# One accumulation for the attention and HGRN output products, both GLA heads of a pair together, value products in batches of two, and stores issued with a margin

## The chip, the cores and the metric

The kernel runs on one core of one Trainium2 chip. The metric is the device time of the program in microseconds (us), the median of several runs. PE is the matrix engine, DVE the vector engine, ACT the scalar engine, POOL the GpSimd engine; SP issues the DMAs.

## The reference

A two-layer encoder over 1024 tokens of width 1024. In each layer one input projection feeds four branches (attention with rotary positions, HGRN2, Mamba-2 SSD, GLA), each 512 wide and multiplied by a SiLU gate. One output projection and a layer norm close the layer.

```python
for i in range(DEPTH):
    h = jnp.einsum('bsd,dn->bsn', x, w_in[i])
    (a_q, a_k, a_v, a_z, h_q, h_ff, h_fb, h_i, h_z,
     s_xbc, s_dtf, s_dtb, s_z, g_q, g_k, g_v, g_lf, g_lb, g_z) = split_columns(h, IN_SPLITS)
    y_a = attention_branch(a_q, a_k, a_v, a_z, ...)   # 8 heads of 64, 2 key heads, softmax
    y_h = hgrn2_branch(h_q, h_ff, h_fb, h_i, h_z, ...)   # gated scan, 4 heads, key width 128
    y_s = ssd_branch(s_xbc, s_dtf, s_dtb, s_z, ...)   # conv of 5, chunked scan, 8 heads
    y_g = gla_branch(g_q, g_k, g_v, g_lf, g_lb, g_z, ...)   # gated scan, 4 heads, key width 64
    mixed = jnp.concatenate([y_a, y_h, y_s, y_g], axis=-1)
    out = jnp.einsum('bsn,nd->bsd', mixed, w_out[i])
    x = layer_norm(DEEPNORM_ALPHA * x + out, ln_g[i], ln_b[i])
```

All scans run forward and backward and are summed. GLA's four heads have keys of width 64, so two of them share a tile of 128 partitions: such a pair is what the code calls `p`, and `hh` is the head within it.

## The kernel before

Features lie on the partitions and tokens along the free dimension, in two halves (`hf`) of 512 tokens. A float32 product of the projections is split into a high and a low part (`xh`, `xl`, `whi`, `wlo`; `mxh`, `mxl` for the output projection) and done as three products of 128x512: high with high, high with low, low with high. A weight tile comes by DMA (`wraw`, three buffers), ACT makes `whi` from it and POOL makes `wlo` (`w_conv`, line 458).

Nothing is placed by a scheduler outside the file. `Plan` (line 125) holds a table of costs in ns for each engine, `run` (line 548) goes through the program with it and decides at each step what is emitted next. There are two kinds of items: *fill* items (`F`: input projections and output projections, a queue in order) and *mix* items (`M`, on twelve lanes: attention, scans, norms, loads). An item is a generator; what it yields says what its next step waits for: tiles, free buffers (`"k2:12"` is twelve free buffers of the pool `k2`, 62 of 128x512; `k4`, eight of 128x1024; `"P"` and `"A"` are PSUM banks) or a condition. `run` takes the mix step that is ready first by the plan's clock; where none is ready, or where PE has streamed fewer columns in the present 3413 ns than `share` of 3072 (`behind`, line 143; `share` is the third number of `KNOBS`), it takes a fill step instead. So fill work is what stands between the steps of a chain, and the order is fixed when the program is built: each engine runs its list in order and waits by semaphores.

The stages of a layer, in order: the projections of attention, then attention (`a_qprep`, `a_s`: scores `S` and their maximum `mx` on DVE; `a_e`: scores again as `ST`, exponentials `Pt` on ACT, their running sum `psum` on POOL, line 1621; `a_pv`: products `O` with the values, one key block `st` at a time, line 1651); HGRN's four heads (`h_proj` as fill, `h_mix`); SSD (`spec_proj` and `spec_post` make the decay rates for SSD and GLA, `s_conv`, `s_w`, `s_mix`); GLA's two pairs (`g_load`, `g_mix`); the layer norm. HGRN and GLA share `tree` (line 605: seven levels, each a step on DVE and ACT between products `lv`) and `scan_unit` (line 678), whose `rest` sums three products per chunk `c` of 128 tokens into `ot`: the values with `AT`, and the states `Sb` and `Sf` with `QP`. It does so for one head `hh` after the other (lines 725 to 738); for GLA the second kind of product uses 64 rows of the array.

The output projection is cut by branch `br` (0 attention, 1 HGRN, 2 SSD, 3 GLA) and half. `out_prep` (line 845) loads a branch's result and splits it, at most two of these at a time (`len(mixes) < 2`); `out_proj` (line 868) is fill: four weight tiles `jp`, each for two output tiles `j`, each 12 products of 128x512 (`oproj`). Each branch is added on DVE to the accumulator `acc` in SBUF. Branch 3 takes `A` banks, the others (`OBIG`) a `P` bank.

SP issues all DMAs in order. A result is not stored at once: `store` puts it in a list, and `flush` (line 423) issues those whose source is ready by the plan's clock, ahead of the next step; a load of stored data flushes what it needs.

Of the kernel before, what the change touches and what calls it, by code (L numbers as in the profile page):

```python
# [15 lines left out]
ALU = mybir.AluOpType  # L16
# [21 lines left out]
OA = ((0, 0), (1, 0), (0, 1), (1, 1), (2, 0), (2, 1), (3, 0), (3, 1))  # L38
# [75 lines left out]
TICK, TICK_COLS = 3413.3, 3072.0  # L114
LAT = {("dve", "dve"): 127.0, ("act", "dve"): 131.0, ("dve", "act"): 128.0, ("dve", "pool"): 155.0, ("pool", "dve"): 134.0,
# [9 lines left out]
class Plan:  # L125


    def __init__(self):
# [9 lines left out]
        self.port = []  # L138

# [115 lines left out]
class Eng:  # L255
# [3 lines left out]
    def __getattr__(self, fn):  # L259
        real = getattr(self._e, fn)  # L260

        def call(*args, **kw):
# [7 lines left out]
            if fn == "matmul":  # L270
                cost = n / 2.4 + 13.5 if args[1].dtype == F32R else n / 0.6 + 8.0
                cols = n * args[1].ap[0][1] / 128.0 * (1 if args[1].dtype == F32R else 2)
                if n == 32:
                    cost = 34.0
                elif out.ap[0][1] == 64:
                    cost /= 2
# [28 lines left out]
def hybrid_trunk(ctx, tc, xT_d, wt_d, wo_d, pk_d, w2_d, gain_d, masks_d, imask_d, tri_d, ident_d, rope_d, lnr_d, out_d):  # L305
# [372 lines left out]
    def scan_unit(halves, nh, emit_o):  # L678
# [38 lines left out]
        def rest():  # L717
# [4 lines left out]
            for hf in (0, 1):  # L722
                u = un[hf]
                yield from states(hf, 0, Sf[hf * 4], Sf)
                for hh in range(nh):
                    p = slice(hh * kk, (hh + 1) * kk)
                    yield ["A:1"] + u["AT"] + [S[hf * 4 + c] for S in (Sf, Sb) for c in range(4) if S[hf * 4 + c] is not None]
                    ot = tps("ot")
                    for c in range(4):
                        g = hf * 4 + c  # L730
                        parts = [(halves[hf][1][hh][:, ck(c)], u["AT"][hh][:, ck(c)])]
                        if Sb[g] is not None:
                            parts.append((Sb[g][p, :], u["QP"][p, 1, ck(c)]))
                        if Sf[g] is not None:
                            parts.append((Sf[g][p, :], u["QP"][p, 0, ck(c)]))
                        for n, (a, b) in enumerate(parts):
                            mm(ot[:, ck(c)], a, b, n == 0, n == len(parts) - 1)
                    yield from emit_o(hf, hh, ot)
# [44 lines left out]
    def layer(li):  # L783
# [84 lines left out]
        def out_proj(br, hf):  # L868
# [1103 lines left out]
```

## Time and profile before

| | us |
|---|---|
| median of 3 runs (2640.47 to 2652.59) | 2641.02 |
| the profiled execution | 2644.85 |
| its span, from the first to the last instruction | 2643.0 |
| DVE busy | 1588.1 (60%) |
| POOL busy | 1227.7 (46%) |
| ACT busy | 1092.9 (41%) |

Stages of the first layer by the trace, from the span's start: projections for attention to 130 us, attention to 400, HGRN to 726, SSD to 990, GLA to 1190, the rest of the output projection and the norm to 1350. The second layer follows in the same way and ends at 2643. A row of the view by stretches gives, for each stretch, the busy time and the instructions of each engine, the clock granted to PE (1.00 is full, 0.50 half) and the share of the DMA engines. In the view by groups a row reads: line, engine, operation, output<-inputs, form, count, busy time, mean ns of one, idle time of the engine before them and what ended it. A float32 product that isn't split stands as two records. Nearly every instruction has line 299, the helper that records them, so groups are told apart by their tiles.

### The profile page before, as it was taken

The page shows a single profiled execution, that of the slowest core. Times are in us where ns is not written, and L with a number is a line of the kernel's source. Part 1 is how long each engine was busy: PE and PEld are TensorE (multiplying, and loading weights), DVE is VectorE, ACT ScalarE, POOL GpSimd, SP SyncE. Part 2 cuts the span into 40 slices and gives each one's busy share as a digit, 9 for nine tenths or more (in the row PEclk, how much of TensorE's full clock was granted, in tenths as well). Part 3 has the DMA queues.
Part 4 walks back from the last instruction along what each step waited for, and adds up shares of the span by engine and source line. Part 5 has one row for each costly group of instructions (what it writes and reads, how often), then busy time and mean ns, then how long its engine had stood idle before and what let it go on. Part 6 is the DMA issues. An engine that isn't in the chain of part 4 may idle for free. (4 is left out here: it accounts for less than half of the span.)

```text
span 2643.0 us, 46508 instructions
## 1 busy us (share of the span) xinstructions
PE 2481.6 (94%) x18352; PEld 1855.2 (70%) x18352; DVE 1588.1 (60%) x2895; ACT 1092.9 (41%) x2100; POOL 1227.7 (46%) x932
## 2 busy tenths in 40 slices
PE   8999899999989997889989999999999999988996
PEld 6855457777877886667777655577777787866675
DVE  2574520565489778863555745206664898868737
ACT  4445453332464433334344444533334543433342
POOL 3556663223335446423554566642223454564334
PEclk9999999999989998989999999999999899999998
DMA  6311112011137447622343111120111365676232
GB/s 210 100 48 52 36 43 66 33 53 49 46 112 252 148 148 256 218 71 89 100 162 112 64 38 48 51 68 29 57 41 46 131 237 152 189 262 203 79 104 100
DMA packets 170173, 284.38 MB, mean 108 GB/s; under 512 B 17780, under 2 KB 43380, under 8 KB 169956
## 3 DMA queue, kind: packets, MB, share of 16 engines
q1 hardware_dynamic: 169956, 281.41, 32.5%
q8 instruction: 145, 2.38, 0.4%
q14 instruction: 72, 0.59, 0.1%
HBM read 205.39 MB, written 75.96 MB: 106 GB/s over the span
## 5 line engine op out<-in xcount | busy, mean ns | idle before, releaser
L299 POOL TENSOR_TENSOR wlo<-wraw,whi 128x512 fp32r<-128x512 f32 x372 | 509.9, 1391 | 585.3 <-ACT whi L299 528.7
L299 PE MATMUL proj<-xh,whi 128*128 128x512 f32 x1056 | 429.4, 407 | 4.7 <-DVE u L299 4.7
L299 PE MATMUL proj<-xl,whi 128*128 128x512 f32 x1056 | 415.1, 393 | 0.0
L299 PE MATMUL projh<-xh,whi 128*128 128x512 f32 x704 | 287.8, 409 | 10.4 <-ACT whi L299 9.6
L299 POOL TENSOR_TENSOR psum<-psum,Pt 128x1024 f32<-128x1024 f32 x96 | 228.6, 2381 | 128.2 <-ACT Pt L299 123.1
L299 ACT CAST whi<-wraw 128x512 fp32r<-128x512 f32 x372 | 216.6, 623 | 165.0 <-DMA wraw<-in_wt 63.7
L299 PE MATMUL proj<-xh,wlo 128*128 128x512 f32 x1056 | 281.0, 400 | 0.0
L299 PE MATMUL projh<-xl,whi 128*128 128x512 f32 x704 | 280.2, 398 | 0.3 <-DVE xl L299 0.3
L299 PEld LDWEIGHTS proj<-xh,whi 128*128 128x128 f32 x1056 | 199.6, 189 | 49.1 <-ACT ga L299 5.5
L299 PE MATMUL oproj<-mxh,whi 128*128 128x512 f32 x512 | 217.8, 425 | 15.9 <-ACT whi L299 9.2
L299 PEld LDWEIGHTS proj<-xl,whi 128*128 128x128 f32 x1056 | 200.2, 190 | 37.2
L299 PEld LDWEIGHTS proj<-xh,wlo 128*128 128x128 f32 x1056 | 192.6, 188 | 41.3 <-issue 2.1
L299 ACT ACTIVATE Pt<-ST 128x512 f32<-128x512 f32 x256 | 151.1, 597 | 135.6 <-PE ST L299 133.8
L299 PE MATMUL oproj<-mxl,whi 128*128 128x512 f32 x512 | 206.2, 403 | 0.0
L299 PE MATMUL projh<-xh,wlo 128*128 128x512 f32 x704 | 193.9, 398 | 0.0
L299 DVE TENSOR_REDUCE mx<-S 128x1 f32<-128x1024 f32 x128 | 151.9, 1218 | 53.5 <-PE S L299 52.4
L299 DVE TENSOR_TENSOR QP<-QP,T 128x512 f32<-128x512 f32 x168 | 144.7, 861 | 48.4 <-PE lv L299 47.5
L299 PEld LDWEIGHTS projh<-xh,whi 128*128 128x128 f32 x704 | 134.8, 192 | 54.9 <-issue 13.4
L299 ACT COPY M<-C 128x256 f32<-128x256 f32 x168 | 69.4, 415 | 241.2 <-DVE C L299 241.2
L299 PE MATMUL oproj<-mxh,wlo 128*128 128x512 f32 x512 | 152.7, 412 | 4.1 <-POOL wlo L299 4.1
L299 PEld LDWEIGHTS projh<-xl,whi 128*128 128x128 f32 x704 | 134.9, 192 | 27.5 <-DVE xl L299 1.5
L299 PEld LDWEIGHTS projh<-xh,wlo 128*128 128x128 f32 x704 | 129.0, 189 | 35.3 <-issue 9.7
(241 smaller groups left out, 4602.1 us busy)
## 6 DMA issues: line engine op xcount, KB each, us to landing
wraw<-in_wt SPq DMA_DIRECT2D x244, 256.0 KB
wraw<-in_wo SPq DMA_DIRECT2D x128, 256.0 KB
hdr<-zs SPq DMA_DIRECT2D x64, 256.0 KB
zs<-hdr SPq DMA_DIRECT2D x64, 256.0 KB
bc<-dr SPq DMA_DIRECT2D x64, 256.0 KB
yld<-yd SPq DMA_DIRECT2D x56, 256.0 KB
hdr<-sp SPq DMA_DIRECT2D x40, 256.0 KB
yd<-o SPq DMA_DIRECT2D x40, 256.0 KB
```

The source lines that it names most:

```text
L299: return real(*args, **kw)
```

## The change

The parts, by the functions they touch:

- `out_proj` takes a tuple of branches. Branches 0 and 1 of a half go into one accumulation in one `P` bank, with two weight tiles per `jp`, and one addition to `acc` where there were two. Branch 3 takes a `P` bank too, and `acc` is added after both output tiles of a `jp`. `out_prep` lets four branches be prepared (`NMIX`).
- `scan_unit`'s `rest` takes both heads of a pair in each chunk.
- `a_pv` takes two key blocks per step (`PVB`); `a_e` sums the exponentials on DVE; the number of live `Pt` tiles is `NP` for the first four query blocks and `NQ` = 4 after; `a_pv` has a lane of its own.
- HGRN's first projections may start after query block 4 (`H0`) where it was 6, and a head's mix no longer waits for the last `aP`, but for two free `k4` buffers.
- `spec_proj` comes right after the attention projections and `spec_post` then, where both came after HGRN's projections.
- The first GLA pair starts after SSD's third head pair (`sm2`) where it was the fourth, the second after the fourth where it was the first pair's first half.
- `flush` issues a store only once its source has been ready for 2000 ns by the plan's clock (`LATE`).
- The plan: 95 ns on PE for each change of form (`SWITCH`), new costs for POOL and for small products, `share` 1.0 where it was 0.5.

```diff
-KNOBS = ((None, 100, 0.5),)
-OA = ((0, 0), (1, 0), (0, 1), (1, 1), (2, 0), (2, 1), (3, 0), (3, 1))
+KNOBS = ((None, 100, 1.0),)
+OA = (((0, 1), 0), ((0, 1), 1), ((2,), 0), ((2,), 1), ((3,), 0), ((3,), 1))
+PVB = 2
+H0, NQ = 4, 4
+NMIX = 4
+SWITCH = 95.0
+LATE = 2000.0
...
-                cost = 155 + 2.09 * n + (120 if fn == "tensor_copy" else 0)
+                cost = 160 + 2.17 * n + (120 if fn == "tensor_copy" else 0)
+            if name == "pe":
+                form = (args[1].ap[0][1], out.ap[0][1]) if fn == "matmul" else (128, 128)
+                if form != self._p.form:
+                    cost += SWITCH
+                    self._p.form = form
...
-            if every or key in keys or plan.ready.get(src.tensor.name, 0.0) <= now:
+            if every or key in keys or plan.ready.get(src.tensor.name, 0.0) + LATE <= now:
...
+                yield [f"A:{nh}"] + u["AT"] + [S[hf * 4 + c] for S in (Sf, Sb) for c in range(4) if S[hf * 4 + c] is not None]
+                ots = [tps("ot", hold=True) for hh in range(nh)]
+                for c in range(4):
+                    g = hf * 4 + c
+                    Ss = [(S[g], d) for S, d in ((Sb, 1), (Sf, 0)) if S[g] is not None]
+                    for hh in range(nh):
+                        mm(ots[hh][:, ck(c)], halves[hf][1][hh][:, ck(c)], u["AT"][hh][:, ck(c)], True, False)
+                    for S, d in Ss:
+                        for hh in range(nh):
+                            p = slice(hh * kk, (hh + 1) * kk)
+                            mm(ots[hh][:, ck(c)], S[p, :], u["QP"][p, d, ck(c)], False, d == Ss[-1][1])
...
-                yield [lambda: len(mixes) < 2, f"k2:{OP[li]}"]
+                yield [lambda: len(mixes) < NMIX, f"k2:{OP[li]}"]
...
+        def out_proj(brs, hf):
+                mix = [mixes[br, hf] for br in brs]
+                for jp in range(4):
+                    for i in range(len(brs)):
+                        ws.append(w_get())
...
+                        for jj in range(2):
+                            o, s0 = hs(ps, jj), jj * 128
+                            for n in range(4):
+                                w = whi[:, n * 256 + s0:n * 256 + s0 + 128]
+                                mm(o, w, mix[i][n][0], i == 0 and n == 0, False)
+                                mm(o, w, mix[i][n][1], False, False)
...
-                    yield [lambda: live[0] < NP[li], "k4:1"]
+                    yield [lambda: live[0] < (NP[li] if ti < H0 else NQ), "k4:1"]
...
-                        tt(gp, acc_s, acc_s, P, ALU.add)
+                        tt(ve, acc_s, acc_s, P, ALU.add)
...
+                for s0 in range(0, 8, PVB):
+                    sts = range(s0, s0 + PVB)
+                    yield [lambda: all((ti, st) in pts for st in sts)]
...
+        F(f"sp{li}", spec_proj, after=x1 + [f"set{li}"], ws=[wsrc("sp")])
+        M(f"spp{li}", spec_post, needs=[f"sp{li}"], lane=3)
-        F(f"sp{li}", spec_proj, after=[f"hp{li}3"], ws=[wsrc("sp")])
-        M(f"spp{li}", spec_post, needs=[f"sp{li}", f"hm{li}2"], lane=3)
...
-            M(f"gp{li}{p}", g_load(p), needs=names + ([f"sm{li}3"] if p == 0 else [f"gn{li}0"]), lane=8)
+            M(f"gp{li}{p}", g_load(p), needs=names + ([xlast, f"sm{li}2"] if p == 0 else [f"sm{li}3"]), lane=8)
```

How it moves instructions, at three places. The first is PE in the first layer's GLA, at the sums `ot` of the first pair's first half (the number behind a name is the buffer's). Before, in one of the two heads (`V_9402`), each chunk's product with `AT` is followed by that head's two products with the states:

```order
L299 MATMUL ot_10619<-AT_10267,V_9402 128x128
L299 MATMUL ot_10619<-QP_9410,S_10533 128x128
L299 MATMUL ot_10619<-QP_9410,S_10561 128x128
L299 MATMUL ot_10619<-AT_10267,V_9402 128x128
L299 MATMUL ot_10619<-QP_9410,S_10531 128x128
L299 MATMUL ot_10619<-QP_9410,S_10563 128x128
```

In the changed program the same place reads:

```order
L312 MATMUL ot_10605<-AT_10228,V_9271 128x128
L312 MATMUL ot_10606<-AT_10234,V_9273 128x128
L312 MATMUL ot_10605<-QP_9292,S_10419 128x128
L312 MATMUL ot_10606<-QP_9292,S_10419 128x128
L312 MATMUL ot_10605<-QP_9292,S_10520 128x128
L312 MATMUL ot_10606<-QP_9292,S_10520 128x128
```

Two products of full height now stand together, and the 64-row products of the two heads alternate between two `ot` tiles.

The second place is PE between that pair's sums `ot` of the first and of the second half (`gss` is the sum of squares of a finished head, `kst`, `P` the next states, `lv` a level of the other half's tree). Before, from the second head's sum on:

```order
L299 MATMUL lv<-QP,M 32x32 x32
L299 MATMUL gss<-sq,ones 128x512
L299 MATMUL oproj<-mxh,whi 128x512
L299 MATMUL oproj<-mxl,whi 128x512
L299 MATMUL kst<-ident,M 128x128
L299 MATMUL kst<-ident,C 128x128
L299 MATMUL kst<-ident,M 128x128
L299 MATMUL kst<-ident,C 128x128
L299 MATMUL lv<-QP,M 32x32 x32
L299 MATMUL P<-V,KST 64x128 x6
L299 MATMUL oproj<-mxh,whi 128x512
L299 MATMUL oproj<-mxl,whi 128x512
```

In the changed program, from the products `P` of that place on:

```order
L312 MATMUL P<-V,KST 64x128 x6
L312 MATMUL oproj<-mxh,wlo 128x512 x2
L312 MATMUL oproj<-mxh,whi 128x512
L312 MATMUL oproj<-mxl,whi 128x512
L312 MATMUL oproj<-mxh,whi 128x512
L312 MATMUL oproj<-mxl,whi 128x512
L312 MATMUL oproj<-mxh,whi 128x512
L312 MATMUL oproj<-mxl,whi 128x512
L312 MATMUL oproj<-mxh,whi 128x512
L312 MATMUL oproj<-mxl,whi 128x512
L312 MATMUL oproj<-mxh,wlo 128x512 x4
L312 MATMUL lv<-QP,M 32x32 x32
```

Where two products of the output projection stood between two steps of the chain, fourteen stand now.

The third place is DVE in the first layer's attention, around a query block's score maxima `mx`. Before:

```order
L299 TENSOR_REDUCE mx<-S 128x1 x4
L299 TENSOR_SCALAR qhl<-mx 128x4
L299 SCALAR_TENSOR_TENSOR qhl<-mx,qhl 128x4
L299 TENSOR_REDUCE mx<-S 128x1 x3
L299 TENSOR_TENSOR ya<-O,rz 128x512
L299 TENSOR_REDUCE mx<-S 128x1
```

In the changed program:

```order
L312 TENSOR_REDUCE mx<-S 128x1
L312 TENSOR_TENSOR psum<-Pt 128x1024
L312 TENSOR_REDUCE mx<-S 128x1
L312 TENSOR_TENSOR psum<-psum,Pt 128x1024
L312 TENSOR_REDUCE mx<-S 128x1
L312 TENSOR_TENSOR ya<-O,rz 128x512
L312 TENSOR_REDUCE mx<-S 128x1
```

A sum of 128x1024 now stands between two maxima on the same engine.

More of the change, by code (lines that the diff above doesn't have):

```diff
@@ L138, in __init__ @@
         self.port = []
+        self.form = None
     def warm(self, t):
@@ L273, in call @@
                 if n == 32:
-                    cost = 34.0
+                    cost = 28.0
                 elif out.ap[0][1] == 64:
@@ L724, in rest @@
                 yield from states(hf, 0, Sf[hf * 4], Sf)
-                for hh in range(nh):
[L726 to L738, printed above, removed]
+                yield [f"A:{nh}"] + u["AT"] + [S[hf * 4 + c] for S in (Sf, Sb) for c in range(4) if S[hf * 4 + c] is not None]
[9 more added lines that the diff above has]
+                            mm(ots[hh][:, ck(c)], S[p, :], u["QP"][p, d, ck(c)], False, d == Ss[-1][1])
+                del Ss, S
+                for hh in range(nh):
+                    yield from emit_o(hf, hh, ots[hh])
                 u.clear()
@@ L866, in out_prep @@
             return gen
[L868 removed]
+        def out_proj(brs, hf):
             def gen():
[L870 to L871 removed]
+                mix = [mixes[br, hf] for br in brs]
+                first, final = 0 in brs, 3 in brs
                 for jp in range(4):
[L873 to L885 removed]
+                    ws, xr = [], []
+                    for i in range(len(brs)):
+                        ws.append(w_get())
+                        if i == 0:
+                            yield [ws[0][0]] + [m[0] for m in mix[0]] + [m[1] for m in mix[0]]
+                            if first:
+                                flush([("xd", hf)])
+                                for j in (jp * 2, jp * 2 + 1):
+                                    xr.append(k2("xr"))
+                                    sy.dma_start(xr[-1], xsrc[j * 128:(j + 1) * 128, hf * HALF:(hf + 1) * HALF])
@@ new lines, in gen @@
+                    for jj in range(2):
+                        j, o = jp * 2 + jj, hs(ps, jj)
+                        if first:
+                            a = k2("acc")
+                            acc[j, hf] = a
+                            ve.scalar_tensor_tensor(out=a, in0=xr.pop(0), scalar=ALPHA, in1=o, op0=ALU.mult, op1=ALU.add)
+                        else:
+                            a = acc[j, hf]
+                            tt(ve, a, a, o, ALU.add)
+                        if final:
+                            summed.add((j, hf))
@@ L927, in layer, with o_src @@
+                    drop(ps)
+                    del ws, whi, wlo
+                for br in brs:
+                    del mixes[br, hf]
+            return gen
+        def o_src(brs):
+            return [wo_d[li, br, jp] for jp in range(4) for br in brs]
         h_in, o_h, lbs = {}, {}, {}
@@ L1265, in gen @@
                     yield None
-                sd["g", g] = (Cc, CB, Bt)
+                sd["g", g] = (Cc, Bt)
+                sd["cb", g] = CB
             return gen
@@ L1459, in emit_o @@
                 ac.copy(o, ot)
+                drop(ot)
                 res = []
```

112 lines of the change are left out of this document (34 added, 78 removed).

## The prediction

> **What bounds the kernel now.** I read the page's first part, then the stretches, then PE's waits, then single rows. The page's first rows:
>
> ```profile
> span 2643.0 us, 46508 instructions
> PE 2481.6 (94%) x18352; PEld 1855.2 (70%) x18352; DVE 1588.1 (60%) x2895; ACT 1092.9 (41%) x2100; POOL 1227.7 (46%) x932
> ```
>
> PE is busy 94% of the span, and the two programs hold the same products. So the change can act on four things: what a product costs beside its neighbours, PE's idle time (161 us here), the time in which PE's clock is lower, and the program's ends. Where idle time and clock are lost is read from the stretches:
>
> ```profile
> core 0: us, PE busy (x) PEld busy (x) DVE busy (x) ACT busy (x) POOL busy (x), PEclk, DMA share, GB/s
> 130.00:400.00 270.00, 250.36 (x1046) 143.20 (x1045) 137.38 (x155) 130.72 (x218) 164.47 (x84) 0.98 0.15 47
> 462.00:726.00 264.00, 261.39 (x2767) 206.12 (x2766) 144.50 (x312) 93.41 (x192) 80.16 (x76) 1.00 0.14 45
> 726.00:765.00 39.00, 32.34 (x269) 23.16 (x268) 32.22 (x45) 28.53 (x44) 17.78 (x16) 0.82 0.26 95
> 990.00:1190.00 200.00, 167.29 (x2370) 126.24 (x2372) 152.74 (x292) 68.16 (x131) 96.34 (x83) 0.87 0.55 182
> 1450.00:1720.00 270.00, 259.67 (x1125) 158.21 (x1123) 139.23 (x169) 132.96 (x225) 168.97 (x86) 0.98 0.16 50
> ...
> 2046.00:2112.00 66.00, 61.46 (x422) 47.20 (x421) 57.02 (x81) 40.41 (x62) 26.45 (x22) 0.90 0.35 121
> 2310.00:2460.00 150.00, 129.89 (x1738) 98.19 (x1736) 113.23 (x206) 50.92 (x96) 75.84 (x65) 0.92 0.63 208
> ```
>
> A stretch loses its idle time, and its length times what is missing of the clock. By that, attention loses 20 + 5 = 25 us in layer 1 (first row) and 10 + 5 = 15 in layer 2 (fifth); HGRN 2.6 of 264 (second); the stretch with `spec_post` 7 + 7 = 14 (third) and 5 + 7 = 12 (sixth); GLA 33 + 26 = 59 (fourth) and 20 + 12 = 32 (last). HGRN runs the same tree as GLA and loses 1%: what differs is the fill work between the steps. GLA's 91 us are the largest loss of any stage, and no single cause makes them, as PE's longest waits in the first GLA stretch show (total, times, longest):
>
> ```profile
> PE oproj L299 <- ACT whi L299: 9.2, 1, 9.2
> PE lv L299 <- POOL ks L299: 3.7, 1, 3.7
> PE lv L299 <- DVE QP L299: 3.1, 4, 1.1
> PE oproj L299 <- POOL wlo L299: 2.8, 2, 2.3
> ```
>
> **The change part by part.** The sum is made against the profiled execution, 2644.85 us, which stands 3.8 above the median of the runs, 2641.02.
>
> *A, changes of form on PE.* Counted in the two programs' order, 798 neighbours on PE differ in form (rows times columns of the array) before and 668 after: `O` goes in batches of two, `ot` with both heads, and fill lands elsewhere. The price, from three products behind a 64*64 one:
>
> ```profile
> 1109.08 0.50 PE L299 MATMUL oproj<-mxh,whi 128*128 128x512 f32 x1
> 1109.42 0.40 PE L299 MATMUL oproj<-mxl,whi 128*128 128x512 f32 x1
> 1109.65 0.39 PE L299 MATMUL oproj<-mxh,whi 128*128 128x512 f32 x1
> ```
>
> The first, which follows the change, takes 0.34 to the next start, the second 0.23. I take 0.1 for a change (the difference is 0.11 here): 130 x 0.1 = **-13 us**. This is PE's own list, so nothing hides it.
>
> *B, the 64-row products of two heads in turn.*
>
> ```profile
> 1159.05 0.71 PE L299 MATMUL ot<-QP,S 64*128 64x128 f32 x4
> 1159.69 0.49 PE L299 MATMUL ot<-AT,V 128*128 128x128 f32 x2
> ```
>
> ```profile
> L299 PE MATMUL ot<-QP,S 64*128 64x128 f32 x224 | 45.2, 320 | 0.0
> L299 PE MATMUL lv<-QP,M 128*64 128x64 f32 x512 | 21.9, 228 | 0.0
> L299 PE MATMUL lv<-QP,M 64*64 64x64 f32 x512 | 12.2, 230 | 5.2 <-DVE QP L299 3.8 <-ACT M L299 1.1 <-DVE near L299 0.4
> ```
>
> Four records of one head take 0.64 to the next start, 0.54 without the change of form; 224 records are 56 such fours, 30 us. Whether the upper and the lower 64 rows run side by side on 128 columns no row shows. The nearest is `lv`: as many records take 12.2 us where both row halves are used and 21.9 where one is all 128 rows, a ratio of 0.56. I take that: 0.44 x 30 = **-13 us**, from 0 to -15. The page TensorEngine Tiling (Array Packing) of the Trainium skill, section Restrictions and Gotchas, says that different row tiles must not use one PSUM bank at the same time; the two heads write two `ot` tiles, so by that page they may overlap, and a full halving would make the term -15.
>
> *C, GLA with more fill between its steps.* In layer 1 the first pair's steps had 2 to 4 output products between them, and 186 stood in one block behind GLA; after, 4 to 18 stand between them and 134 in the block. One `oproj` is a step of 0.23 us (above), so a gap of 2 covers 0.5 us and one of 14 covers 3.2, which is more than most of the waits above. HGRN, with 4 to 16 between its steps, loses 1%; at that rate GLA's 350 us would lose 4, the best end, -87. The other end is 0, as DVE is busy 153 of 200 and 113 of 150 us there. Layer 2 had 2 to 20 already. I take 59 to 19 in layer 1 and 32 to 20 in layer 2: **-52 us**. The merging of branches 0 and 1 goes in here; the 32 additions to `acc` that it saves (0.68 each) cost PE nothing now, since DVE waits for them:
>
> ```profile
> L299 DVE TENSOR_TENSOR acc<-acc,oproj 128x512 f32<-128x512 f32 x96 | 62.5, 680 | 64.3 <-PE oproj L299 63.7
> ```
>
> *D, `spec_post` moved into attention.* Its old stretches lose 14 + 12 = 26 us. The chain through ACT and DVE is as long in its new place, where projections stand between its steps. I take half: **-12 us**, from -26 to 0.
>
> *E, attention.* 112 sums of 128x1024 leave POOL (2.38 each, 266 us) and go to DVE. The rows, in ns least, median and most: the sum on POOL with those who waited for it, the same form on DVE (the first `QP`), and the score maximum:
>
> ```profile
> L299 POOL TENSOR_TENSOR psum<-psum,Pt x96: 2337/2377/2611, 147.4 to 1734.9; 128x1024 f32<-128x1024 f32 x96
> ...
> who waited for it (us, times):
>   ACT rz L299: 3.4, 3
>   ACT Pt L299: 0.9, 1
> ```
>
> ```profile
> L299 DVE TENSOR_TENSOR QP<-q,T x24: 1216/1222/2292, 472.4 to 2482.0; 128x1024 f32<-128x1024 f32 x24
> ```
>
> ```profile
> L299 DVE TENSOR_REDUCE mx<-S 128x1 f32<-128x1024 f32 x128 | 151.9, 1218 | 53.5 <-PE S L299 52.4
> ```
>
> Nobody waited 5 us for `psum`, so a faster sum gains little. DVE gets 56 x 1.22 = 68 us per layer, on 137 of 270; the stage also gets longer, as the block of bare projections behind it shrinks from 238 to 114 products (28 us) in layer 1. The cover is DVE's idle half, and the fill between two `S`. What is queued behind a sum on DVE is the maximum of a score tile (1.22), for which PE waits before the next-but-one `S`. At best the stage's 25 + 15 us go; for the worse end see the rivals. I take **0**. The lower limit on `Pt`, the earlier start of HGRN, the added waits for free buffers, and the plan's new constants only set this order, and have the same two ends.
>
> *Stores with a margin: 0.* SP waits long for the sources of stores, with weight loads queued behind:
>
> ```profile
> SPq L299 <- POOL wlo L299: 810.3, 181, 17.2
> SPq L299 <- DVE zs L299: 522.7, 45, 30.7
> ```
>
> But of this PE sees only waits for `whi`, whose one large case (9.2 us) is in C. Loads that flush their own store keep doing so. I keep -10 and +10 as ends.
>
> *F, the end: +2 us.* The last four transposes of 128x128 no longer stand among products: 12 follow the last `oproj`, where 8 did. With the copies (0.28 each, partly side by side) that is about 2 us:
>
> ```profile
> L299 ACT COPY xt<-outT 128x128 f32<-128x128 f32 x64 | 12.4, 280 | 26.0 <-PE outT L299 25.8
> ```
>
> The sum: -13 - 13 - 52 - 12 + 0 + 0 + 2 = -88; 2644.85 - 88 = 2557, and 3.8 lower against the median: **2553 us**.
>
> **The rivals.**
>
> *GLA's chain is bound by DVE, not by missing fill.* For it: DVE is busy about 76% there, and two pairs side by side load it more. Against: HGRN's tree is covered with 4 to 16 products. C would be -15: **2590**.
>
> *The sums on DVE hold up the score maxima (slower).* One queue, one place: each of the 128 `S` tiles finds a sum of 1.22 us ahead of its maximum, PE has two such tiles, and the fill isn't enough. If all are exposed that is 156 us on 2553: **2709**; from 83 tiles on the change is slower by over 0.5%. POOL can make it worse, as single rows of `QP` with the same two inputs reach 2.29, 1.07 above the median. Against it: DVE waits 52 us for `S` now, and the median of that row stands at its least. The page SBUF — State Buffer of the Trainium skill, section Who interferes with whom, says that a DVE instruction with two SBUF inputs and a GpSimd one that reads SBUF exclude each other for the whole instruction; the tail of `QP` agrees.
>
> *The change doesn't do what it says.* Its order is better by the plan's clock, and on the chip the waits reappear elsewhere, attention losing 15 us more: A, B and F stay, 2553 + 52 + 12 + 15 = **2632**, within 0.5%.
>
> *Everything is covered.* C at -87 and 20 of attention's 40 us: **2498**.
>
> **How the numbers follow.** My forecast has 0.55 (its own range is 2525 to 2590), the DVE-bound GLA 0.22, everything covered 0.06, no effect 0.09, slower 0.08. The range of 2510 to 2628 takes in the first two with the bounds of A, B, D and the stores; it leaves out the last two and half of the third, 2 in 10. About 0.5% (13 us) is what a measurement of this kernel can tell from no change. Faster: 0.55 + 0.22 + 0.06 = 0.83; within 0.5%: 0.09; slower: 0.08.
>
> **What would show it.** A: steps behind `O` and `ot` fewer, PE's busy sum lower at a full clock. B: the 64-row `ot` records at about half of their 45 us of busy time. C: in GLA's stretches a clock above 0.95 and idle time under 10%. D: no stretch behind HGRN at 0.82 or 0.90. E: PE's waits for DVE `mx`; if they pass 40 us in total, the step is wrong. The forecast as a whole falls if attention's stretches lose over 40 us each.

## The result, and the profile after

The changed kernel takes **2578.73 us** (median of 4 runs, 2576.8 to 2583.47), the kernel before beside it 2642.85 (2640.47 to 2652.59). The ratio is 0.9753, with a 95% interval of 0.9725 to 0.9782: 64 us faster. Predicted were 2553 us, in a range of 2510 to 2628. The profiled execution took 2583.47 us, 61.4 less than that of before (2644.85).

The first rows of the page of the changed kernel:

```profile
span 2581.4 us, 46457 instructions
PE 2439.2 (94%) x18352; PEld 1843.5 (71%) x18352; DVE 1637.3 (63%) x2975; ACT 1075.9 (42%) x2090; POOL 963.8 (37%) x820
```

PE does the same number of products in 42 us less of busy time, and its idle time fell from 161 to 142 us. POOL lost the 264 us of the sums, DVE got them at half the price. Where the time went is read by stages; the view by stretches of the kernel before, over attention (two rows) and over SSD and GLA together (two rows), which is now cut at the stages' own ends:

```profile
113.00:412.00 299.00, 279.36 (x1179) 162.70 (x1177) 151.88 (x175) 142.07 (x239) 181.39 (x93) 0.98 0.15 46
1444.00:1734.00 290.00, 279.67 (x1212) 170.61 (x1210) 144.76 (x176) 143.30 (x242) 183.21 (x94) 0.98 0.16 51
...
785.00:1231.00 446.00, 406.47 (x3720) 321.64 (x3718) 337.21 (x639) 170.71 (x325) 212.23 (x178) 0.94 0.53 174
2102.00:2554.00 452.00, 422.68 (x3838) 334.20 (x3837) 350.98 (x652) 177.47 (x340) 221.87 (x188) 0.97 0.55 181
```

The same of the changed kernel, with the last stretch of HGRN, where `spec_post` was (740 and 2003), and GLA alone (988 and 2279) among them:

```profile
137.00:457.00 320.00, 312.75 (x1384) 201.85 (x1386) 214.43 (x259) 164.62 (x284) 75.41 (x52) 0.99 0.20 63
1411.00:1724.00 313.00, 308.40 (x1367) 198.22 (x1367) 214.94 (x259) 166.78 (x283) 77.45 (x52) 0.99 0.20 65
...
740.00:779.00 39.00, 36.25 (x258) 29.10 (x257) 28.74 (x53) 14.93 (x27) 8.75 (x10) 0.91 0.42 140
2003.00:2069.00 66.00, 62.70 (x503) 51.57 (x503) 54.18 (x101) 28.37 (x50) 15.36 (x15) 1.00 0.36 126
...
797.00:1188.00 391.00, 362.43 (x3594) 287.87 (x3594) 285.01 (x578) 150.71 (x291) 201.78 (x173) 0.96 0.55 183
2069.00:2489.00 420.00, 383.68 (x3655) 304.42 (x3653) 305.47 (x587) 153.65 (x297) 211.45 (x179) 0.94 0.56 178
...
988.00:1188.00 200.00, 179.38 (x2582) 135.48 (x2582) 141.15 (x251) 75.71 (x141) 101.70 (x92) 0.94 0.50 167
2279.00:2489.00 210.00, 187.05 (x2586) 141.10 (x2584) 135.14 (x249) 68.47 (x128) 93.16 (x87) 0.91 0.43 142
```

A stretch loses its idle time and its length times what is missing of the clock, as in the prediction. Attention lost 26 and 16 us and now loses 10 and 8. SSD and GLA together lost 66 + 43 = 109 us and now lose 44 + 62 = 106: layer 1 won 22, and layer 2 lost 19 again. So the stage that the prediction counted on most gave next to nothing, and attention, counted at nothing, gave 24 us.

The rest of the gain is in what products cost. In the view by groups, of the changed kernel:

```profile
L312 PE MATMUL O<-Pt,Vt 128*64 128x512 f32 x512 | 125.7, 612 | 0.0
L312 PE MATMUL ot<-AT,V 128*128 128x128 f32 x256 | 48.3, 290 | 2.1 <-DVE S L312 2.0
L312 PE MATMUL ot<-QP,S 64*128 64x128 f32 x224 | 22.4, 315 | 0.0
```

The 64-row records of `ot` are busy 22.4 us, where they were 45.2, though one of them lasts as long as before (315 ns, where it was 320): they run two at a time. By the page TensorEngine Tiling (Array Packing) of the Trainium skill, section Restrictions and Gotchas, different row tiles must not use one bank at the same time; the two heads write two tiles, and the trace agrees that these overlap. Those of `O` take 125.7, where they took 137.8:

```profile
L299 PE MATMUL O<-Pt,Vt 128*64 128x512 f32 x512 | 137.8, 624 | 7.0 <-ACT Pt L299 5.1 <-DVE zs L299 1.9
```

The sums on DVE, and the maxima beside them (ns least, median and most):

```profile
L312 DVE TENSOR_TENSOR psum<-psum,Pt x96: 1207/1225/2303, 167.0 to 1722.2; 128x1024 f32<-128x1024 f32 x96
...
L312 DVE TENSOR_REDUCE mx<-S x128: 1205/1216/1226, 139.3 to 1669.7; 128x1 f32<-128x1024 f32 x128
```

The median is what was predicted, and of the tail of 2303 little comes into the mean (1279). PE's longest waits for its chains, and that for `mx` (total, times, longest):

```profile
PE yd L312 <- POOL Wm L312: 12.3, 2, 7.5
...
PE P L312 <- ACT KST L312: 9.8, 3, 4.9
...
PE lv L312 <- DVE near L312: 9.5, 4, 4.4
...
PE S L312 <- DVE mx L312: 0.9, 3, 0.4
```

The sums stand between the maxima, and PE waits 0.9 us for these in the whole program. What waits there are belong to SSD (`yd`) and GLA (`P`, `lv`).

**A second measure.** The experiments were judged by PE's time split in two. Products are sorted by their tiles, their form, and whether the next one has the same form. The price of a sort is the mean distance from one start to the next, over the lower nine tenths of those without a gap and at a full clock. The sum of all prices is PE's *list*; what PE takes beyond it is its *loss* (idle time and slow clock together). By this, the list fell from 2309 to 2267 us, and the loss from 306 to 283: in attention from 70 to 50 (43 to 26 in layer 1, 28 to 24 in layer 2), in SSD and GLA from 143 to 142 (84 to 64, 60 to 78), elsewhere from 92 to 91. One execution is uncertain here: the profiled one of the changed kernel is the slowest of its four (2583.47 us), and the three kernels below that keep its order and GLA's work lose 130 to 135 us in SSD and GLA. So some 10 of the 142 us belong to that execution.

### The profile page after: what moved, and what is told of

The parts are those of the page before. It is cut to its first block, busy times and chain, and to the rows that moved or that the text cites. A ratio compares the mean times of both kernels' runs of the same rounds, so it can differ in the third digit from the quotient of the medians.

```text
span 2581.4 us, 46457 instructions
## 1 busy us (share of the span) xinstructions
PE 2439.2 (94%) x18352; PEld 1843.5 (71%) x18352; DVE 1637.3 (63%) x2975; ACT 1075.9 (42%) x2090; POOL 963.8 (37%) x820
## 5 line engine op out<-in xcount | busy, mean ns | idle before, releaser
L312 POOL TENSOR_TENSOR wlo<-wraw,whi 128x512 fp32r<-128x512 f32 x372 | 518.9, 1416 | 672.3 <-ACT whi L312 609.4
L312 DVE TENSOR_TENSOR QP<-QP,T 128x512 f32<-128x512 f32 x168 | 150.1, 894 | 46.3 <-PE lv L312 44.6
L312 DVE TENSOR_TENSOR psum<-psum,Pt 128x1024 f32<-128x1024 f32 x96 | 122.8, 1279 | 63.7 <-ACT Pt L312 62.9
```

What stands on the lines that cost most here:

```text
L312: return real(*args, **kw)
```

## The experiments

All kernels, with the ratio to the kernel before on the same chip, and, from the trace of one execution each, list and loss. "Against" is the difference of ratios times 2641 us: against the changed kernel (0.9753) in the upper rows, against the kernel before in the last two. A difference to the changed kernel is uncertain by some 10 us, since both ratios have intervals of about 0.003 to each side.

| kernel | median, us | ratio (95%) | against | list | loss | of it attention | SSD + GLA |
|---|---|---|---|---|---|---|---|
| before | 2642.85 | 1 | | 2309 | 306 | 70 | 143 |
| changed | 2578.73 | 0.9753 (0.9725 to 0.9782) | | 2267 | 283 | 50 | 142 |
| heads_apart | 2630.29 | 0.9974 (0.9951 to 0.9997) | +58 | 2295 | 297 | 54 | 151 |
| heads_fixed | 2598.72 | 0.9856 (0.9830 to 0.9883) | +27 | 2294 | 266 | 49 | 130 |
| sums_pool | 2585.90 | 0.9812 (0.9786 to 0.9839) | +16 | 2273 | 287 | 62 | 134 |
| sums_fixed | 2608.19 | 0.9882 (0.9855 to 0.9909) | +34 | 2267 | 308 | 81 | 133 |
| gla_old | 2594.77 | 0.9846 (0.9818 to 0.9873) | +25 | 2271 | 290 | 57 | 142 |
| unmerged | 2592.88 | 0.9817 (0.9800 to 0.9833) | +17 | 2272 | 286 | 62 | 135 |
| late0 | 2575.48 | 0.9750 (0.9733 to 0.9766) | -1 | 2266 | 279 | 48 | 136 |
| yld_margin | 2588.24 | 0.9799 (0.9783 to 0.9815) | +12 | 2274 | 276 | 59 | 122 |
| yld_act | 2573.23 | 0.9747 (0.9724 to 0.9770) | -2 | 2268 | 275 | 50 | 135 |
| gla_short_qp | 2568.60 | 0.9733 (0.9707 to 0.9759) | -5 | 2267 | 264 | 50 | 123 |
| before_heads | 2648.56 | 1.0031 (1.0020 to 1.0043) | +8 | 2280 | 332 | 83 | 154 |
| before_sums | 2642.46 | 1.0025 (1.0009 to 1.0040) | +7 | 2312 | 296 | 50 | 155 |

Most of these edits make the plan choose another order from the edit on, for every engine. Four kernels, `heads_fixed`, `sums_fixed`, `yld_act` and `gla_short_qp`, keep the changed kernel's order: the plan reckons as in the changed kernel, and only what is issued differs.

### The two heads

`heads_apart`:

```diff
-                for c in range(4):
...
-                    for S, d in Ss:
-                        for hh in range(nh):
...
+                for hh in range(nh):
+                    p = slice(hh * kk, (hh + 1) * kk)
+                    for c in range(4):
...
+                        for S, d in Ss:
                             mm(ots[hh][:, ck(c)], S[p, :], u["QP"][p, d, ck(c)], False, d == Ss[-1][1])
```

> The changed kernel, with the products of `ot` given one head after the other again (all of the first head's chunks, then all of the second's), two `ot` tiles still held at once. Up to the first layer's GLA the order is that of the changed kernel. Theory (the gain lies in what products cost on PE beside their neighbours: by the mean distances of starts, the 64-row products with the states went from 36 to 16 us, those with `AT` from 37 to 32): 20 to 28 us are lost again, 2599 to 2607 us, and the 64-row `ot` rows are busy 45 us again, from 22. Rival (the gain comes from the new order of fill and chains, and the heads' order is hidden behind GLA's waits): within 8 us of 2579, whatever those rows show.

The list grew by 28 us as the theory has it, but the time by 52 to 58, far above both expectations. Of the rest, 14 us show in the trace as loss of the new order (10 more in the first layer's GLA and 11 in the second's SSD, with some won elsewhere); the two profiled executions are only 42 us apart. Two causes in one number; so the next kernel keeps the order. `heads_fixed` lets the plan reckon with the heads together, holds the products back, and issues them head by head:

```diff
+                pe._held, heads = [], []
...
-                del Ss, S
+                held, pe._held = pe._held, None
+                for hh in range(nh):
+                    for b, (real, args, kw) in zip(heads, held):
+                        if b == hh:
+                            real(*args, **kw)
```

> The changed kernel with its whole order as it is (every other instruction of every engine in its place); only inside each sum `ot` of GLA are the products given one head after the other. It tells the direct cost of the heads' order from what a new plan brings. Theory (the products are on PE's own list, and what they save is saved in the end): 22 to 30 us lost, 2601 to 2609, the 64-row rows busy 45 us. First rival (GLA's waits take it, as in the kernel before with the heads together, where 28 us less of products gave no time): under 10 us lost, below 2589. Second rival (the 51 us that the heads' order cost with a new plan are its own): over 40 us lost, above 2619.

Its group of 64-row products:

```profile
L760 PE MATMUL ot<-QP,S 64*128 64x128 f32 x224 | 41.8, 301 | 0.0
```

They are back at 41.8 us, the list is 27 us longer, and the time 20 (by medians, a little under the expected range) to 27 us (by ratios). What the order of the heads takes off PE's list is saved in the end; the theory holds, and the excess of `heads_apart` was the order. (Its loss of 266 is that of one execution, 5 us below the median.)

`before_heads` does the same part alone, in the kernel before:

```diff
+                ots = [tps("ot", hold=True) for hh in range(nh)]
+                for c in range(4):
...
+                    for S, d in Ss:
+                        for hh in range(nh):
+                            p = slice(hh * kk, (hh + 1) * kk)
+                            mm(ots[hh][:, ck(c)], S[p, :], u["QP"][p, d, ck(c)], False, d == Ss[-1][1])
...
                 for hh in range(nh):
-                    p = slice(hh * kk, (hh + 1) * kk)
...
-                    ot = tps("ot")
...
-                        for n, (a, b) in enumerate(parts):
-                            mm(ot[:, ck(c)], a, b, n == 0, n == len(parts) - 1)
```

> The kernel before, with nothing changed but both heads of a GLA pair in each chunk of `ot`. Theory (this shortens PE's own list by 20 us at the 64-row products and by 7 at those with `AT`): 20 to 30 us faster than the kernel before, 2613 to 2623, the 64-row rows busy 22 us. Rival (in the old order this time lies beside GLA's waits, which take it back): within 10 us of 2643, with the same rows at 22 us.

The rival holds, and more than it said: PE's list is 29 us shorter, and the kernel is 8 us slower (5 to 11). The loss grew by 26 us, half of it not in GLA but in the second layer's attention, where nothing was edited. Its row, beside which the kernel before has 10 us of idle time:

```profile
1419.00:1722.00 303.00, 281.08 (x1197) 165.89 (x1197) 148.75 (x176) 142.39 (x242) 181.15 (x93) 0.98 0.15 47
```

PE is idle for 22 us there; its longest waits are 7.5 us in all for `Pt` and 6.2 for `qhl`, of the kind that the next part follows back. So the same edit is worth 27 us in one order and nothing in another. Which step of the plan loses the time in the old order wasn't followed up.

### The sums

`sums_pool` (the plan knows of it) and `sums_fixed` (it does not):

```diff
-                        tt(ve, acc_s, acc_s, P, ALU.add)
+                        tt(gp, acc_s, acc_s, P, ALU.add)
```

```diff
+    vg = Eng(plan, "dve", nc.gpsimd)
...
-                        tt(ve, acc_s, acc_s, P, ALU.add)
+                        tt(vg, acc_s, acc_s, P, ALU.add)
```

> The changed kernel, with the sums of the exponentials on POOL again. Theory (attention's loss, which fell from 43 to 26 us in layer 1 and from 28 to 24 in layer 2, fell because a sum of 1.2 us frees `Pt` tiles earlier than one of 2.4): 15 to 25 us are lost again, 2594 to 2604 us, and PE waits more in attention. Rival (the batches of two value products and the lower limit on `Pt` did it, and the engine of the sum is free): within 8 us of 2579, attention losing 25 in each layer.

> The changed kernel with its whole order as it is; only the engine of the sums of the exponentials is POOL, at the same places of the program. Theory (a sum of 2.4 us behind others on POOL frees `Pt` later, and PE waits in attention): 10 to 25 us lost, 2589 to 2604, attention's loss up from 26 and 24 us by as much. Rival (the 7 us that the sums on POOL cost with a new plan came from the plan): within 6 us of 2579.

With a new plan 7 (medians) to 16 us (ratios) are lost, between the two expectations, and attention's loss is 62. In the same order 29 to 34 us are lost, more than the theory asked for, and all of it in attention (loss 50 to 81). The two attention stretches of `sums_fixed`:

```profile
137.00:477.00 340.00, 319.68 (x1385) 205.49 (x1386) 182.95 (x203) 165.09 (x285) 201.60 (x108) 0.97 0.18 59
1430.00:1754.00 324.00, 309.93 (x1362) 198.85 (x1364) 175.05 (x203) 166.81 (x285) 202.25 (x108) 0.99 0.19 63
```

Idle time is 20 and 14 us, where it was 7 and 5, and both stages are longer, by 20 and 11 us. PE's longest waits in the first of them (total, times, longest):

```profile
PE ST L312 <- ACT Pt L312: 7.0, 4, 4.5
PE qmT L312 <- DVE qhl L312: 7.0, 7, 2.0
...
PE Z L312 <- POOL psum L312: 0.6, 1, 0.6
```

The waits for `psum` itself are 0.6 us. What costs more are waits for others, and they lead back to DVE. `qhl` is made by two instructions of DVE on four columns; their durations (ns least, median and most), in the changed kernel and then in `sums_fixed`:

```profile
L312 DVE TENSOR_SCALAR qhl<-mx x32: 170/171/1198, 144.8 to 1671.0; 128x4 fp32r<-128x4 f32 x32
```

```profile
L312 DVE TENSOR_SCALAR qhl<-mx x32: 170/530/2349, 145.2 to 1697.8; 128x4 fp32r<-128x4 f32 x32
```

One of them, of the second kind, in `sums_fixed`:

```profile
359.89 2.35 POOL L312 TENSOR_TENSOR psum<-psum,Pt 128x1024 f32<-128x1024 f32 x1
359.99 2.27 DVE L312 SCALAR_TENSOR_TENSOR qhl<-mx,qhl 128x4 fp32r<-128x4 f32 x1
...
362.41 0.50 PE L312 MATMUL qmT<-ident,qhl 128*128 128x128 f32 x4 [1.99 <-DVE qhl L312]
```

An instruction of 0.17 us starts 0.1 us after a sum on POOL, lasts 2.27 us, and ends with it. Of the 64 of both kinds, 22 take over 0.3 us in `sums_fixed` and 5 in the changed kernel, and each of these ends 22 to 32 ns after an instruction of POOL (in `sums_fixed` a sum for 13 of the 22). The longest wait, 4.5 us for `Pt`, has the same source: ACT, which makes `Pt`, stands 6.9 us for `tot`, the end of `spec_post`'s chain on DVE, and from `RA` to `tot` this chain takes 17.9 us in `sums_fixed`, where it took 9.0. PE's waits of `qmT` for `qhl`, 11.3 us in the whole program where they were 1.0, and this one make up 15 of the 22 us by which PE's idle time in attention grew; the rest was not taken apart. In the whole program no `Pt` on ACT is seen to wait for a sum, so what the expectations named, `Pt` tiles that a slower sum frees later, is not what the trace shows. The page SBUF — State Buffer of the Trainium skill states, in the section Who interferes with whom, that DVE and GpSimd (POOL) share a pair of ports, and that of two instructions that both need it the later one is blocked until the first is done. The trace agrees with it in the instructions named here.

`before_sums` is the same edit in the kernel before, to DVE:

```diff
-                        tt(gp, acc_s, acc_s, P, ALU.add)
+                        tt(ve, acc_s, acc_s, P, ALU.add)
```

> The kernel before, with nothing changed but the sums of the exponentials, which go to DVE. Theory (a faster sum frees `Pt` earlier): 10 to 20 us faster than the kernel before, 2623 to 2633 us, its attention losing less than 43 and 28 us. Rival (without the batches and the lower limit the sums stand in front of the score maxima): equal or slower, 2643 to 2665 us, with PE waiting over 10 us for `mx`.

Attention's loss fell from 70 to 50, just as in the changed kernel, without batches and without the lower limit on `Pt`; PE's waits of `qmT` for `qhl` fell from 7.1 us in the kernel before to 0.3. So the engine of the sums is what shortens attention, and it needs no other part. But the kernel is 7 us slower (2 to 11): the loss of SSD and GLA in the new order is 155, where it was 143.

### SSD and GLA: the loss that stays

`gla_old`:

```diff
-            M(f"gp{li}{p}", g_load(p), needs=names + ([xlast, f"sm{li}2"] if p == 0 else [f"sm{li}3"]), lane=8)
+            M(f"gp{li}{p}", g_load(p), needs=names + ([f"sm{li}3"] if p == 0 else [f"gn{li}0"]), lane=8)
```

> The changed kernel, with GLA's first pair starting after SSD's fourth head pair and its second after the first pair's first half, as in the kernel before. Theory (the earlier start brought nothing: SSD and GLA together lost 84 us before and 64 after in layer 1, 60 before and 78 after in layer 2): within 10 us of 2579, layer 1 losing more and layer 2 less. Rival (what was predicted, that the earlier start and the fill around it save GLA's idle time, and something else in layer 2 took it): 25 to 50 us are lost, 2604 to 2629.

25 us were lost (16 by medians), between the two expectations. By the trace SSD and GLA lose 142 us (73 and 68), as much as in the changed kernel's profiled execution and some 10 more than in other executions of its order, so the start decides little of this loss; 4 us more are in the list and 7 in attention.

The changed kernel's longest wait of PE in these stages is 7.5 us for POOL's `Wm`. The timeline around it (start, length, instruction, and in brackets the idle time before it and its releaser), shown for the engines of that chain:

```profile
2261.66 1.85 SPq L312 DMA_DIRECT2D yld<-yd  x4
...
2265.91 0.62 ACT L312 CAST mxh<-yld 128x512 fp32r<-128x512 f32 x1 [4.89 <-DMA yld<-yd]
...
2268.09 0.62 ACT L312 CAST mxh<-yld 128x512 fp32r<-128x512 f32 x1 [1.56 <-DMA yld<-yd]
...
2268.91 1.33 ACT L312 CAST mxh<-yld 128x512 fp32r<-128x512 f32 x2 [0.20 <-DMA yld<-yd]
...
2270.15 0.62 ACT L312 ACTIVATE sq<-u 128x512 f32<-128x512 f32 x1
2270.68 0.61 ACT L312 ACTIVATE bc<-bc 128x512 f32<-128x512 f32 x1
2270.86 1.27 POOL L312 TENSOR_TENSOR ssq<-ssq,sq 128x512 f32<-128x512 f32 x1 [8.32 <-ACT sq L312]
...
2272.09 1.26 POOL L312 TENSOR_TENSOR u<-u,zs 128x512 f32<-128x512 f32 x1
...
2273.32 1.26 POOL L312 TENSOR_TENSOR Wm<-Wm,bc 128x512 f32<-128x512 f32 x1
...
2274.62 1.75 PE L312 MATMUL yd<-Wm,xt 128*64 128x128 f32 x13 [7.50 <-POOL Wm L312]
```

PE is said to wait for POOL. POOL has stood 8.32 us for ACT's `sq`, does two instructions of its list first, and then `Wm`, for which it also needs ACT's `bc`. ACT could have made both earlier, had not four casts `mxh` for the output projection stood ahead of them, waiting for loads that SP issued at 2261.66. The wait belongs to a load of another stage, at the head of ACT's list. Two kernels test that. `yld_margin` moves the casts back:

```diff
                     sy.dma_start(y, ydr[r0:r0 + 128, hf * HALF:(hf + 1) * HALF])
+                    plan.ready[y.tensor.name] += 6000.0
```

> The changed kernel, in which the plan takes a loaded branch result (`yld`) as ready 6 us later, so that its casts `mxh` on ACT come later in ACT's list. Theory (SSD and GLA lose about 142 us whatever their start, because a cast stands first in ACT's list for a load that is late, 7.5, 4.5 and 4.4 us of PE's waits in layer 2 of the changed kernel): the loss of SSD and GLA falls below 125 us, ACT waits under 10 us for `yld` there, and the time is 2555 to 2570 us. Rival (DVE, busy 72 to 91% in these stages, bounds them): the loss stays at 142 within 10 and the time within 8 us of 2579, with the waits at other places.

The step is nearly as expected, the time not. ACT's waits for `yld` in SSD and GLA are down from 17.0 and 30.7 us to 8.0 and 12.3, where under 10 was expected; PE's wait of 7.5 us for `Wm` in layer 2 is gone, and the loss of SSD and GLA is 122. But attention loses 9 us more, the list is 7 longer, and the kernel is 12 us slower. `yld_act` has ACT issue the same loads, in the same order:

```diff
+    sy, sw = Eng(plan, "dma", nc.sync), Eng(plan, "dma", nc.scalar)
...
-                    sy.dma_start(y, ydr[r0:r0 + 128, hf * HALF:(hf + 1) * HALF])
+                    sw.dma_start(y, ydr[r0:r0 + 128, hf * HALF:(hf + 1) * HALF])
```

> The changed kernel with its whole order on PE, DVE and POOL as it is; only the loads of the branch results (`yld`, 56 of 256 KB) are issued by ACT at the same places of the program, not by SP, which stands up to 18.6 us for the buffers of weight loads. Theory (the casts stand on ACT for loads that SP issued late): ACT's waits for `yld` fall from 51 us to under 25, PE's waits of 7.5, 4.5 and 4.4 us in the second layer's SSD and GLA shrink, and 5 to 15 us are won, 2564 to 2574. Rival (the loads are late because the transfers come in bursts that fill the DMA engines, or DVE bounds these stages): within 6 us of 2579, ACT's waits within a third of 51 us.

The rival holds: the same time (ratio 0.9747). ACT waits 47.8 us for `yld` where it waited 51.5, only in more and shorter pieces:

```profile
ACT mxh L312 <- DMA yld<-yd: 47.8, 33, 4.5
```

At the place shown above ACT stands for a weight tile first, issues the loads at 2266.39, and waits 3.96 us for the first of them. So it is not SP's list alone that makes these loads late.

`gla_short_qp` takes work off DVE in GLA's chain:

```diff
+            ve._held = [] if nh == 2 else None
             tt(ve, qa, qa, AV(T, nblk + 1, [[2, ng2], [-nblk - 1, 2], [0, h]]), ALU.mult)
+            ve._held = None
+            if nh == 2:
+                qs = QP[:, 1, 0:64]
+                nc.vector.tensor_tensor(out=qs, in0=qs, in1=AV(T, 0, [[0, 64]]), op=ALU.mult)
```

> The changed kernel with its whole order as it is; only in GLA's tree is the scaling of `QP` on DVE done on 64 columns in place of 512, so that most of `QP` is left without its decay factors. 56 instructions of DVE, one at each level, are shorter by some 0.55 us at least, 31 us in all, on the chain from one level to the next. Theory (GLA's steps are bound by its chain through DVE, which is busy 72 to 79% there): GLA's loss of 46 and 55 us falls by 15 us or more in total, and 12 to 31 us are won, 2548 to 2567. Rival (fill covers the level-to-level steps, and GLA's loss sits at single waits behind loads and other stages' work, and in the clock that follows them): under 8 us won, above 2571, with PE's waits of 4 us and more where they were.

The rows of that scaling in the changed kernel, and then in this one (HGRN's and GLA's):

```profile
L312 DVE TENSOR_TENSOR QP<-QP,T 128x512 f32<-128x512 f32 x168 | 150.1, 894 | 46.3 <-PE lv L312 44.6
```

```profile
L312 DVE TENSOR_TENSOR QP<-QP,T 128x512 f32<-128x512 f32 x112 | 87.4, 780 | 21.9 <-PE lv L312 20.4
...
L673 DVE TENSOR_TENSOR QP<-QP,T 128x64 f32<-128x64 f32 x56 | 25.9, 462 | 28.9 <-PE lv L312 28.6
```

150.1 - 87.4 - 25.9 = 37 us of DVE are gone, all on the way from one level to the next. GLA's loss is 81 us in the trace, where it was 101 in the changed kernel's execution and 89 to 94 in `heads_fixed`, `sums_fixed` and `yld_act`; the time fell by 5 (ratios, within their intervals) to 10 us (medians). A part of DVE's time in the chain seems to be exposed, less than a third of it by the medians, but the difference is not clear of the uncertainty of 10 us; the long waits stayed (7.0 us for `Wm`, 5.7 for `KST`). Neither expectation is met fully, and the rival is the nearer one.

The last two undo parts that the prediction held for nearly free:

```diff
-OA = (((0, 1), 0), ((0, 1), 1), ((2,), 0), ((2,), 1), ((3,), 0), ((3,), 1))
+OA = (((0,), 0), ((1,), 0), ((0,), 1), ((1,), 1), ((2,), 0), ((2,), 1), ((3,), 0), ((3,), 1))
```

> The changed kernel, with attention's and HGRN's output products in accumulations of their own (32 additions to `acc` more on DVE, two more uses of a bank per pair of tiles). Theory (the merging gives nothing, as DVE's additions are beside PE's products): within 8 us of 2579. Rival (32 additions of 0.68 us, 22 us, at a time when DVE is busy 70 to 90%, do cost): 12 to 25 us lost, 2591 to 2604.

```diff
-LATE = 2000.0
+LATE = 0.0
```

> The changed kernel, with the stores issued as soon as the plan has their source ready (no margin). Theory (PE sees none of SP's waits for the sources of stores): within 8 us of 2579, SP waiting more for the sources. Rival (SP standing for a source keeps weight and result loads behind it late): 12 us or more lost, over 2591, and more of ACT's waits for loads.

Without the merging 14 to 17 us are lost, the number that the rival gave, but not where it put them: SSD and GLA, where the additions stand, lose 135, no more than with it, and attention of layer 2, which has none, 12 us more. It is again a new order, and what the merging itself is worth stays open. Without the margin for stores the time is the same (ratio 0.9750), as predicted: SP waits 368.5 us for DVE's `zs` and not 308.8, and PE sees nothing of it.

## Why the prediction was right, and where it was not

The direction was right and the median lies in the range, 26 us above the forecast. That it is so near is in part luck: C and D promised 62 us too much, and A, B and E together 36 too little. The terms against what list, loss and the program's end measured, in us:

| term | predicted | measured |
|---|---|---|
| A and B, what products cost | -13 - 13 | -42 |
| C, GLA | -52 | -1 (SSD and GLA) |
| D, `spec_post` | -12 | -1 (everything but attention, SSD and GLA) |
| E, attention | 0 | -20 |
| F, the end | +2 | +3 (from PE's last product to the last instruction, 22.7 to 25.5) |
| sum | -88 | -61 |

The measured terms add up to the 61.4 us between the two profiled executions.

**A and B** were right in their mechanism, and together too small. The distances between starts show the 64-row products with the states at 15.7 us where they were at 36.1, but these 20 us hold 32 of the 130 changes of form and are not B alone. For B itself, eight records of both heads now take 0.64 us to the next start (1089.64 to 1090.28 in the changed kernel), as four of one head did: a full halving, where I took the 0.56 of `lv`. Inside a head's products one start follows another by 0.11 us; half of that for 224 records is -12, close to the forecast. A is the one that was mis-sized. These rows of the kernel before show what the prediction left out:

```profile
481.51 0.39 PE L299 MATMUL proj<-xh,whi 128*128 128x512 f32 x1
481.74 0.39 PE L299 MATMUL proj<-xl,whi 128*128 128x512 f32 x1
482.06 0.46 PE L299 MATMUL lv<-QP,M 128*32 128x32 f32 x32
```

The product ahead of a change takes 0.32 us to the next start and not 0.23. The prediction read the price only at the product behind the change, 0.11; with the 0.09 ahead of it a change costs 0.2, and 130 of them -26, twice the term. With -12 that makes -38 of the -42 measured; the other 4 are spread over many sorts and were not followed up.

**C failed**, and it is the step that put the forecast too low. Its base was too large: the stretches that were taken for GLA, from 990 and from 2310 us on, begin in SSD, whose products `yd` run to 1030 and 2340. The first two rows are these ends of SSD in the kernel before, the others GLA from its own start to its own end:

```profile
990.00:1032.00 42.00, 28.17 (x152) 23.08 (x151) 37.19 (x72) 14.84 (x31) 24.33 (x19) 0.84 0.76 233
2310.00:2342.00 32.00, 25.22 (x136) 19.70 (x135) 26.95 (x45) 10.54 (x21) 20.07 (x17) 0.89 0.71 223
...
1032.00:1231.00 199.00, 178.12 (x2489) 132.05 (x2487) 131.08 (x255) 70.33 (x130) 85.51 (x81) 0.91 0.45 152
2342.00:2554.00 212.00, 193.48 (x2591) 144.06 (x2590) 139.75 (x266) 76.23 (x142) 92.49 (x88) 0.96 0.48 160
```

SSD lost 31 of the 91 us, the one wait of 9.2 us for `whi` among them, and GLA alone lost 39 + 27 = 66. And I took GLA's loss to be a lack of fill between the steps of its chain. The changed kernel has that fill, some 450 output products in GLA of either layer (where there were about 360 and 460), and still idles for 10 and 11% of it at a clock of 0.94 and 0.91, a loss of 33 + 42 us; both signs that I had named (above 0.95, under 10%) are missing. In all fourteen kernels SSD and GLA together lose between 122 and 155 us, whatever the start of the pairs, the merging, the margins or the engine that issues the loads. What the trace shows instead are a few waits of 4 to 8 us in each layer, at other places in each order; the one followed back stood behind a load for another stage on ACT. The two kernels that act on that place did not tell more: one came out slower in a new order, the other the same; and 37 us less of DVE gave 5 to 10. No single cause was found, and why the sum stays is open.

**D** was half right: the places ahead of HGRN's end lost 14 and 12 us, and at about the same distance from that end 6 and 3 are lost now. But the chain now starts among the projections ahead of attention, whose loss rose from 25 to 32 us, and HGRN's stage as a whole won only about 7 (58 to 51). I had reckoned that half would be given back; it was nearly all. That the chain is what costs the projections 7 us was not tested.

**E** was mis-sized. I read that nobody waited for `psum`, and concluded that a faster sum gains little. In the same order the slower sum costs 29 to 34 us, with 0.6 us of waiting for `psum` in the first attention stage: its price lies, for the most part, in the instructions of DVE that are lengthened while a sum runs on POOL, and in PE's waits behind them. The kernel before shows it too: 24 of its 64 instructions for `qhl` take over 0.3 us, up to 2.36, and each ends within 35 ns after an instruction of POOL. I had kept the 40 us of attention as the best end, and set the value at the wrong one.

**Stores and F** came out as predicted.

**The rivals.** The sums did not hold up the maxima: 0.9 us of waits in all. GLA bound by DVE gives a number near the result (2590), but was at most partly the reason: of the DVE time that could be taken from its chain, less than a third came out. That the waits reappear elsewhere, the third rival, is what happened to C alone: the layers' 22 won and 19 lost.

**The parts do not add up.** In the changed order the heads are worth 20 to 27 us and the sums 29 to 34, together about what the whole change gives; in the order before, with a new plan, each is worth nothing. Undoing one part of four with a new plan (heads, sums, start, merging) costs 58, 16, 25 and 17 us by the ratios, 116 in all, where the whole is 65. A new order moved the loss of attention by up to 13 us (`before_heads`), and that of SSD and GLA by 12 (`before_sums`), without an edit there.

## What to carry to other kernels

Where an order is computed, keep it and change only what is issued, so that one edit gives one number; the same edit came out 31 us dearer with a new plan for the heads, and 18 cheaper for the sums. An engine for whose results nobody waits can still set the time, by lengthening what runs beside it: compare the least and the most duration of one instruction on its neighbour, and look at what ended just before the long ones. And a stage that loses time to many short waits of different origin does not become free when fill is put between its steps.

## What the runs showed of the hardware that was not expected

The granted clock of one and the same program differs between runs, and its time with it: in one session the kernel before took 2628.8 us at a mean clock of 0.975 and 2647.2 at 0.966. That is 18 us between two runs of one kernel, as much as most of the single parts here are worth, so that a single profile tells where time is lost but not by how much two kernels differ.

A small instruction of DVE can last as long as a large one of POOL. The instructions that make `qhl` take 0.17 us alone and up to 2.36 beside POOL, whose sum of 128x1024 takes 2.4; in the kernel before, the changed kernel and `sums_fixed` together 51 of 192 take over 0.3 us, and all of them end 21 to 35 ns after an instruction of POOL. The maxima `mx`, 1205 to 1226 ns in all three, are not lengthened.

Two 64-row products on the two halves of the array cost together what one does, their changes of form included: 45.2 to 22.4 us of busy time, with 315 ns for one of them, where it was 320. And a change of form costs at both of its sides: a product of 128x512 takes 0.23 us to the next start, 0.32 ahead of a change and 0.34 behind one.
